# A gate product computed by four seven-product chains, with residual and embedding stored apart

## The chip, the cores and the metric

The kernel runs on one core of a Trainium2 chip. The metric is the device time of one execution in microseconds (us), the median of several executions. Before the change it is 1686.71 us (three executions, 1683.85 to 1688.95).

TensorE (PE) multiplies and accumulates into PSUM, which has eight banks of 128 x 512 float32. VectorE (DVE), ScalarE (ACT) and GpSimd (POOL) do the elementwise work. SyncE (SP) issues all DMAs here. The engines run side by side and wait for each other by semaphores.

## The reference

One layer of an encoder, with x of 1024 tokens by 1024 channels. The first sub-layer (a gated recurrence and an attention, both projected and merged) ends in `x1`. What the change concerns comes after that:

```python
x1  = layer_norm(DN_ALPHA * x + merged @ w_out, ln1_g, ln1_b)
up  = causal_depthwise_conv(x1 @ w_up, conv_w, conv_b)        # w_up: 1024 x 5632
c_val, c_gate = jnp.split(up, 2, axis=-1)
ffn = (jax.nn.gelu(c_gate) * c_val) @ w_down                  # 2816 x 1024
ple = (p_i @ w_pe) * jax.nn.sigmoid(x1 @ w_pg)                # w_pg: 1024 x 1024
return layer_norm(DN_ALPHA * x1 + ffn + ple, ln2_g, ln2_b)
```

`ple` is the per-layer embedding, and `sigmoid(x1 @ w_pg)` its gate.

## The kernel before

**Layout.** Activations lie transposed: a block of 128 channels on the partitions, 1024 tokens along the free axis. A matmul multiplies a 128 x 128 weight block with a 128 x 512 half of a block. Float32 accuracy comes from splitting each operand into a high part (a cast on ACT, line 87) and a low part (a subtraction on DVE, line 88), and from three matmuls for each product of blocks (`mm3`, lines 101 to 103).

**Stages around the change,** in the order of the trace (us from the start of the span):

1. `w_out_half` (784 to 875): the output projection, then `ln_gen` normalises `x1` half by half (512 tokens each). The second half's statistics are computed while `pe_part` runs.
2. `pe_part` (875 to 900): `p_i @ w_pe`, 96 matmuls, copied by ACT into eight tiles `pl`. Behind it stand the last small matmuls of the normalisation (`l11pr`, line 822). From these DVE scales the eight blocks `R(j)` of the second half (line 824), ACT applies gain and bias (line 864, in `x1_emit`), and each block is split (lines 87 and 88). The quadrants of `x1` are called 11, 12 (first 512 tokens, lower and upper four channel blocks), 21 and 22 (second 512 tokens).
3. `pg_part` (900 to 988): the gate, `x1 @ w_pg`. For each of eight channel blocks j and two token halves it accumulates eight `mm3`, 384 matmuls in all. ACT takes the sigmoid (line 931), DVE multiplies it into `pl` (line 932), adds `ALPHA * R(j)` (line 934) and SP writes the sum to DRAM as `rd[j]` (line 935). Beside it `x1_sums` makes four combinations of `x1`'s quadrants for each of four k (`s1`, `s3` on POOL, lines 876 and 878; `s2`, `s4` on DVE, lines 877 and 879) and splits them. The eight weight tiles of `w_pg` are split whole by `load_w` (line 97).
4. The chains `Up` (988 to 1411): 22 chains for `x1 @ w_up`. A chain computes a 2 x 2 arrangement of blocks with seven products (numbers 1 to 7) instead of eight, each of four `mm3` (12 matmuls). Its weight combinations are made on POOL (line 989: three subtractions and later a fourth) from two loaded tiles `ra`, `rb` into a single buffer `ta`, and each of seven weight tiles is split by ACT and DVE. `BANK` gives the PSUM bank of a product: 1, 6, 5 and 3 accumulate in one of four banks "a", 2 in one of three "b", 7 and 4 in the only bank "e". Products of neighbouring chains alternate in the list `seq`; a weight tile is formed `AHEAD` = 5 products before its use. Of the quadrants, the products use 11, 12, 22 and the four sums; 21 is used by `pg_part` alone.
5. The chains `Down` (1398 to 1616): `ffn`, in two groups of four chains. At the passage from `Up` to `Down`, `hooks` load the gated activations (`gr`, line 1109) and the residuals back from DRAM (`reload`, line 1165: `rr` from `rd`, two at a time), split them and make the sums of the new operands (`su`, `st` on POOL, lines 1143 and 1155). DVE then adds each finished product into `rr` (line 1102).
6. A last layer norm.

**Order and memory.** The order on TensorE is written out by hand; on the other engines a scheduler places each instruction in a list when the kernel is built, by its own estimate of when it is ready. Each engine and the SP queue work through their list in order. Large tiles come from one pool of 39 (`gp`: `R`, `pl`, split quadrants, sums, activations), weight tiles from a pool of 6 (`w`), raw weight tiles from 5 (`wr`), 128 x 512 temporaries from 6 (`hp`). A tile waits until the tile that had its place is done with.

Of the kernel before, what the change touches and what calls it, by code (L numbers as in the profile page):

```python
# [37 lines left out]
def layer_kernel(ctx, tc, xT, pT, w_in, w_a, w_b, w_out, w_up, w_dn, w_down, w_pe, w_pg,  # L38
# [872 lines left out]
    pp, pe_u, pl, last_pg = [], [], [], {}  # L911
# [11 lines left out]

    def pg_part(j, u, hf):
        cs = slice(hf * 512, hf * 512 + 512)
        ps = psS.tile([P, 512], F32, tag="s", name=f"pg{j}{hf}")
# [10 lines left out]
    def x1_sums(k):
        q = lambda j, hf: R(j)[:, hf * 512:hf * 512 + 512]
        sums(xf, k, q(k, 0), q(k + 4, 0), q(k, 1), q(k + 4, 1), f"x{k}")

    with tc.manual_schedule(engines={mybir.EngineType.PE}):
        w_out_half(0, {})
        l0 = ln_gen(R, 0, 512, x1_emit, "l10")
        next(l0)
        step = lambda g: (lambda: next(g, None))
        pre = {(0, 3): step(l0), (3, 2): step(l0), (4, 0): step(l0)}
        for i in range(4):
            src, lst, nm = ((pT[i], pp, f"p{i}") if i < 2 else (w_pe[i - 2], pe_u, f"pe{i}"))
            pre[i + 3, 4] = lambda src=src, lst=lst, nm=nm: lst.append(load_g(src, nm))
        wg = w_out_half(1, pre, ((w_pg[0], "pg0"), (w_pg[1], "pg1")))  # L950
        psD.release()
        psA.release()
        psS = tc.alloc_tile_pool(name="psS", bufs=4, space=PSUM, reuse_waits="tile")
        l1 = ln_gen(R, 512, 512, x1_emit, "l11")
        next(l1)
        for j in range(8):
            pe_part(j)
            if j in (1, 6, 7):
                next(l1, None)
        for k in range(4):  # L960
            x1_sums(k)
# [532 lines left out]
```

## Time and profile before

| | |
|---|---|
| median of three executions | 1686.71 us (1683.85 to 1688.95) |
| the profiled execution | 1684.51 us, of which the span from first to last instruction is 1682.7 us |
| TensorE busy | 1631.2 us (97%), mean granted clock 0.988 of full speed |
| VectorE, ScalarE, GpSimd busy | 1098.9 us (65%), 696.9 us (41%), 378.3 us (22%) |
| DMA | 123.7 MB, 74 GB/s in the mean |

A row of the profile that groups instructions gives line, engine, operation, output and inputs, shape and count, then the busy time in us and the mean of one in ns, and then the idle time of the engine just ahead of them with what ended it. Matmuls overlap in the pipeline, so the time of one (389 ns) is more than the distance from one start to the next. A granted clock of 1.00 is 2.4 GHz, 0.50 is 1.2 GHz.

### The profile page before, as it was taken

To read this page: it belongs to the slowest core of one execution; us is meant where nothing else is said; L and a number is where in the kernel's file an instruction comes from. 1 tells how busy PE (TensorE), PEld (TensorE's weight loads), DVE (VectorE), ACT (ScalarE), POOL (GpSimd) and SP (SyncE) were. 2 spreads that over 40 slices of the span, in tenths; PEclk is the share of its full clock that TensorE was granted. 3 is DMA by queue.
4 is the path that set the end of the run, shared out by engine and by line. 5 is a ranking of instruction groups with operands and counts; after the bars stand their busy time and mean duration, and the time that the engine had idled before them with its cause. 6 is when DMAs were issued, how large, how long until landed. Compare 5 with 4: busy or idle time off the path is not lost.

```text
span 1682.7 us, 21558 instructions
## 1 busy us (share of the span) xinstructions
PE 1631.2 (97%) x8388; PEld 1387.2 (82%) x8388; DVE 1098.9 (65%) x1545; ACT 696.9 (41%) x1189; POOL 378.3 (22%) x316
## 2 busy tenths in 40 slices
PE   7999999999999999999999999999999998898997
PEld 6889888889988888888878888888888886686896
DVE  5786867776576423325686647777777777767646
ACT  5555554542232321222356325554455544333313
POOL 0222222221012000000343132223322233222123
PEclk9999999999999999999999999999999998999999
DMA  6100000101011111114230132222222224331312
GB/s 229 38 26 26 26 26 26 38 26 38 27 38 38 38 50 50 51 38 164 99 127 11 65 123 76 83 80 101 75 76 88 82 103 161 135 132 69 118 43 100
DMA packets 37637, 123.72 MB, mean 74 GB/s; under 512 B 4128, under 2 KB 6816, under 8 KB 37536
## 3 DMA queue, kind: packets, MB, share of 16 engines
q1 hardware_dynamic: 37536, 122.35, 20.4%
q8 instruction: 66, 1.08, 0.3%
q14 instruction: 35, 0.29, 0.1%
HBM read 102.41 MB, written 19.92 MB: 73 GB/s over the span
## 4 chain that ended last, share of the span: by engine, by line
PE 84%; DVE 9%; issue 2%; DMA 2%; ACT 2%; POOL 1%; SPq 0%; POOLq 0%; DVEq 0%; ACTq 0%
PE sau L101 5%; PE sau L102 5%; PE sau L103 5%; PE seu L101 2%; PE seu L102 2%; PE seu L103 2%; PE av L431 2%; PE pi_gb L101 2%; PE pi_gb L103 2%; PE pi_gb L102 2%; PE pg L103 2%; PE pg L102 2%; PE pi_gt L103 2%; PE pi_gt L101 2%; PE pg L101 2%
## 5 line engine op out<-in xcount | busy, mean ns | idle before, releaser
L404 POOL TENSOR_TENSOR be<-be,f 128x127 f32<-128x127 f32 (+3 forms) x64 | 79.3, 1244 | 268.7 <-DVE f L402 232.9
L989 POOL TENSOR_TENSOR tau<-rbu 128x512 f32<-128x512 f32 x44 | 59.1, 1344 | 234.6 <-DVE w7u L88 214.1
L402 DVE TENSOR_TENSOR_SCAN f<-f 128x128 f32<-128x128 f32 (+3 forms) x64 | 90.3, 1421 | 27.9 <-ACT f L398 27.6
L398 ACT ACTIVATE f<-z 128x512 f32<-128x512 f32 (+2 forms) x96 | 47.6, 495 | 28.7 <-PE z L397 28.1
L88 DVE TENSOR_TENSOR wtl<-tr,wth 128x512 fp32r<-128x512 f32 (+1 forms) x80 | 48.9, 627 | 12.3 <-ACT wth L87 11.7
L788 POOL TENSOR_TENSOR l10sa<-r,r 128x512 f32<-128x512 f32 x1 | 1.3, 1284 | 233.3 <-DVE r L899 233.3
L87 ACT CAST wth<-tr 128x512 fp32r<-128x512 f32 (+1 forms) x80 | 43.5, 556 | 21.9 <-PE tr L420 20.4
L101 PE MATMUL pi_gb<-xh,wh_gb 128*128 128x512 f32 x128 | 51.5, 403 | 0.0
L103 PE MATMUL wo<-mm,wl_wo 128*128 128x512 f32 x128 | 50.0, 391 | 1.5 <-DVE wl_wo L97 1.5
L101 PE MATMUL wo<-mm,wh_wo 128*128 128x512 f32 x128 | 50.4, 394 | 0.0
L103 PE MATMUL pi_gb<-xh,wl_gb 128*128 128x512 f32 x128 | 50.0, 391 | 0.0
L101 PE MATMUL pg<-x,wh_pg 128*128 128x512 f32 x128 | 49.9, 390 | 0.0
L102 PE MATMUL pi_gb<-xl,wh_gb 128*128 128x512 f32 x128 | 49.9, 390 | 0.0
L102 PE MATMUL wo<-mm,wh_wo 128*128 128x512 f32 x128 | 49.8, 389 | 0.0
L103 PE MATMUL pg<-x,wl_pg 128*128 128x512 f32 x128 | 49.8, 389 | 0.0
L102 PE MATMUL pg<-x,wh_pg 128*128 128x512 f32 x128 | 49.8, 389 | 0.0
L101 PE MATMUL pi_gt<-xh,wh_gt 128*128 128x512 f32 x128 | 49.8, 389 | 0.0
L102 PE MATMUL pi_gt<-xl,wh_gt 128*128 128x512 f32 x128 | 49.8, 389 | 0.0
L103 PE MATMUL pi_gt<-xh,wl_gt 128*128 128x512 f32 x128 | 49.8, 389 | 0.0
L1056 DVE SCALAR_TENSOR_TENSOR ov<-hv,cv,ov 128x1023 f32<-128x1023 f32 x22 | 39.7, 1806 | 13.7 <-ACT ov L1055 13.7
L399 ACT ACTIVATE be<-z 128x512 f32<-128x512 f32 (+2 forms) x96 | 47.3, 493 | 2.7 <-POOL be L404 2.6
L420 PE MATMUL tr<-ident,be 128*128 128x128 f32 x288 | 45.6, 276 | 1.8 <-DVE wtl L88 1.0
(674 smaller groups left out, 5554.0 us busy)
## 6 DMA issues: line engine op xcount, KB each, us to landing
rau<-in_w_up SPq DMA_DIRECT2D x22, 512.0 KB, 3.2
rbu<-in_w_up SPq DMA_DIRECT2D x22, 512.0 KB, 3.2
gd<-og SPq DMA_DIRECT2D x22, 512.0 KB, 3.0
gr<-gd SPq DMA_DIRECT2D x22, 512.0 KB, 5.0
wr_wo<-in_w_out SPq DMA_DIRECT2D x16, 512.0 KB, 3.2
wr_gb<-in_w_in SPq DMA_DIRECT2D x8, 512.0 KB, 3.1
wr_gt<-in_w_in SPq DMA_DIRECT2D x8, 512.0 KB, 3.2
r<-in_xT SPq DMA_DIRECT2D x8, 512.0 KB, 7.8
```

The costliest lines, as they stand in the source:

```text
L87: nc.scalar.copy(out=hi, in_=src)
L88: nc.vector.tensor_tensor(out=lo, in0=src, in1=hi.bitcast(F32), op=ALU.subtract)
L101: mm(ps, lhsT=ah, rhs=bh, start=start, stop=False, skip_group_check=more)
L102: mm(ps, lhsT=ah, rhs=bl, start=False, stop=False, skip_group_check=more)
L103: return mm(ps, lhsT=al, rhs=bh, start=False, stop=stop, skip_group_check=more)
L398: nc.scalar.activation(f[:, s0:s1], z[:, :s1 - s0], AF.Sigmoid, scale=-0.125)
L399: nc.scalar.activation(be[:, s0:s1], z[:, :s1 - s0], AF.Sigmoid, scale=0.125)
L402: nc.vector.tensor_tensor_scan(out=f[:, :W][:, ::-1], data0=f[:, :W][:, ::-1], data1=f[:, :W][:, ::-1], initial=1.0, op0=ALU.mult, op1=ALU ...
L404: nc.gpsimd.tensor_tensor(out=be[:, :W - 1], in0=be[:, :W - 1], in1=f[:, 1:W], op=ALU.mult)
L420: nc.tensor.transpose(tr[:, j * P:j * P + P], ws[tt][:, sb * P:sb * P + P], ident)
L989: r, sub = self.raw, lambda o, a, b: nc.gpsimd.tensor_tensor(out=o, in0=a, in1=b, op=ALU.subtract)
L1056: nc.vector.scalar_tensor_tensor(out=o[:, 1:], in0=h[:, :T - 1], scalar=cv[:, c, 1:2], in1=o[:, 1:], op0=ALU.mult, op1=ALU.add)
```

## The change

- `pg_part` is replaced by a class `Pg` of four chains of the same kind as `Up` (chain j makes channel blocks j and j + 4): seven products of 12 matmuls each. Products 1 and 2 of all four chains run right behind `pe_part`, from weights that `load_early` fetches and splits without any combination; the other five go into `seq` ahead of and interleaved with the first `Up` chain.
- The products' sums end in the sigmoid on ACT and the multiplication into `pl` on DVE; three of the four quadrants need one more addition on DVE from PSUM. SP writes the result to a new DRAM tensor `pd`.
- The residual `ALPHA * x1` no longer goes through DVE: `x1_sums` scales each `R(j)` in place on ACT (128 x 1024) and SP writes it to `rd` early. `reload` fetches `rd[j]` and `pd[j]`, and POOL adds them (128 x 1024), eight times.
- Quadrant 21 is no longer split (four casts on ACT, four subtractions on DVE less). `x1_sums` makes all 16 sums first and splits them in the order s2, s3, s1, s4.
- `Chain.form` makes the weight combinations also when product 6 is formed first. The next chain is loaded when product 7 of a `Pg` chain (product 1 of the others) is formed.

```diff
     def x1_emit(j, cs):
...
-        xf[nm, j % 4] = X(f"x{nm}{j % 4}")
-        split_form(xf[nm, j % 4], R(j)[:, cs])
+        if nm != "21":
+            xf[nm, j % 4] = X(f"x{nm}{j % 4}")
+            split_form(xf[nm, j % 4], R(j)[:, cs])
...
-    def pg_part(j, u, hf):
-        cs = slice(hf * 512, hf * 512 + 512)
-        ps = psS.tile([P, 512], F32, tag="s", name=f"pg{j}{hf}")
-        wh, wl = unit_fm(u)
-        for k in range(KB):
-            last_pg[j, hf] = mm3(ps, wh(k), wl(k), *x1_part(k, hf), k == 0, k == KB - 1)
-        sg = H(f"psg{j}{hf}")
-        nc.scalar.activation(sg, ps, AF.Sigmoid)
-        nc.vector.tensor_tensor(out=pl[j][:, cs], in0=pl[j][:, cs], in1=sg, op=ALU.mult)
-        if hf:
-            nc.vector.scalar_tensor_tensor(out=pl[j], in0=R(j), scalar=ALPHA, in1=pl[j], op0=ALU.mult, op1=ALU.add)
-            nc.sync.dma_start(out=rd[j], in_=pl[j])
...
-            if i in (2, 7) and not self.summed:
+            if i in (2, 6, 7) and not self.summed:
...
+    class Pg(Chain):
+        def __init__(self, j):
+            super().__init__(f"p{j}", (w_pg[j], w_pg[j + 4]), 512, xf)
+            self.j = j
+
+        def load_early(self):
+            raw = WR(f"re{self.name}")
+            nc.sync.dma_start(out=raw, in_=self.srcs[0])
+            for i in (1, 2):
+                self.w[i] = W(f"w{i}{self.name}")
+                split_form(self.w[i], raw[:, 512 * i - 512:512 * i])
+
+        def evac(self, i, ps):
+            j = self.j
+            if i in (1, 6, 7):
+                s = H(f"s{i}_p{j}")
+                setattr(self, f"s{i}", s)
+                nc.scalar.copy(out=s, in_=ps)
+                return
+            s, o, h = {2: ("s1", 0, 0), 4: ("s6", 0, 1), 5: ("s7", 4, 1), 3: (None, 4, 0)}[i]
+            t = ps
+            sg = H(f"sg{i}_p{j}")
+            if s:
+                nc.vector.tensor_tensor(out=sg, in0=getattr(self, s), in1=ps, op=ALU.add)
+                t = sg
+            nc.scalar.activation(sg, t, AF.Sigmoid)
+            r = pl[j + o][:, 512 * h:512 * h + 512]
+            nc.vector.tensor_tensor(out=r, in0=r, in1=sg, op=ALU.mult)
+            if i in (4, 3):
+                nc.sync.dma_start(out=pd[j + o], in_=pl[j + o])
+
+    def x1_sums():
...
+        for k in range(4):
...
+            nc.gpsimd.tensor_tensor(out=s1, in0=a21, in1=a22, op=ALU.add)
+            nc.vector.tensor_tensor(out=s2, in0=s1, in1=a11, op=ALU.subtract)
+            nc.gpsimd.tensor_tensor(out=s3, in0=a11, in1=a21, op=ALU.subtract)
+            nc.vector.tensor_tensor(out=s4, in0=a12, in1=s2, op=ALU.subtract)
...
+            for j in (k, k + 4):
+                nc.scalar.activation(R(j), R(j), AF.Identity, scale=ALPHA)
+                nc.sync.dma_start(out=rd[j], in_=R(j))
+        for nm in ("s2", "s3", "s1", "s4"):
+            for k in range(4):
+                xf[nm, k] = X(f"x{nm}{k}")
+                split_form(xf[nm, k], tmp[nm, k])
...
+        pgs = [Pg(j) for j in range(4)]
+        for c in pgs:
+            c.load_early()
+        for j in range(8):
+            pe_part(j)
...
+        x1_sums()
+        for c in pgs:
+            c.prod(1)
+            c.prod(2)
...
         after(nc.sync.dma_start(out=rt[j], in_=rd[j]), gate)
+        ple = G(f"ple{j}")
+        after(nc.sync.dma_start(out=ple, in_=pd[j]), gate)
+        nc.gpsimd.tensor_tensor(out=rt[j], in0=rt[j], in1=ple, op=ALU.add)
...
-    seq = []
-    for n in range(len(chains) + 1):
+    seq = [(pgs[0], 6)]
+    for c, d in zip(pgs, pgs[1:]):
+        seq += [(c, 7), (d, 6), (c, 5), (c, 4), (c, 3)]
+    c, d = pgs[3], ups[0]
+    seq += [(c, 7), (d, 1), (c, 5), (d, 2), (c, 4), (d, 6), (c, 3), (d, 7)]
+    for n in range(1, len(chains) + 1):
```

## Rows read from the trace of the kernel before

**Rows 1.** The page, part 1: busy time, share of the span, instructions
```profile
PE 1631.2 (97%) x8388; PEld 1387.2 (82%) x8388; DVE 1098.9 (65%) x1545; ACT 696.9 (41%) x1189; POOL 378.3 (22%) x316
```
**Rows 2.** By stage: stretch, length, busy time of each engine (count), clock, DMA share, GB/s
```profile
900.50:987.70 87.20, 87.20 (x388) 72.20 (x387) 55.62 (x76) 34.75 (x58) 26.27 (x15) 1.00 0.19 73
```
**Rows 3.** Waits of TensorE, 860 to 1000: who for whom, us, times, longest
```profile
PE wo L103 <- DVE wl_wo L97: 1.5, 1, 1.5
```
**Rows 4.** Timeline of TensorE, ScalarE, VectorE, GpSimd, 899 to 923: start, duration, instruction
```profile
899.72 1.05 PE L822 MATMUL l11pr<-ident,l11ss 128*128 128x128 f32 x8
900.53 0.48 PE L101 MATMUL pg<-x,wh_pg 128*128 128x512 f32 x1
...
901.54 1.52 ACT L864 ACTIVATE r<-r,cl 128x512 f32<-128x512 f32 x2 [1.03 <-DVE r L824]
902.96 1.12 ACT L87 CAST x<-r 128x512 fp32r<-128x512 f32 x2
...
922.38 1.05 ACT L95 CAST wh_pg<-wr_pg 128x1024 fp32r<-128x1024 f32 x1 [3.14 <-PE pg L102]
...
900.81 3.08 DVE L824 TENSOR_TENSOR r<-r,l11pr 128x512 f32<-128x512 f32 x5 [3.62 <-PE l11pr L822]
...
907.34 1.32 POOL L876 TENSOR_TENSOR x0t<-r,r 128x512 f32<-128x512 f32 x1 [9.04 <-ACT r L864]
908.61 1.75 POOL L878 TENSOR_TENSOR x0u<-r 128x512 f32<-128x512 f32 x1
...
916.97 4.62 POOL L878 TENSOR_TENSOR x1u<-r 128x512 f32<-128x512 f32 x1 [4.91 <-DVE x0s L88]
```
**Rows 5.** Timeline of VectorE at 909.5
```profile
909.13 1.78 DVE L88 TENSOR_TENSOR x<-r,x 128x512 fp32r<-128x512 f32 x1
```
**Rows 6.** Groups on VectorE and GpSimd, 1411 to 1426
```profile
L88 DVE TENSOR_TENSOR gl<-gr,gh 128x1024 fp32r<-128x1024 f32 x3 | 6.7, 2288 | 0.0
L88 DVE TENSOR_TENSOR gs<-su,gs 128x512 fp32r<-128x512 f32 x3 | 5.1, 1761 | 0.0
...
L1143 POOL TENSOR_TENSOR su<-gr 128x512 f32<-128x512 f32 x3 | 6.0, 2025 | 0.0
L1155 POOL TENSOR_TENSOR st<-gr,gr 128x512 f32<-128x512 f32 x3 | 5.6, 1902 | 0.0
```
**Rows 7.** Tiles gr and rr: duration ns min/median/max, first and last start
```profile
L88 DVE TENSOR_TENSOR gl<-gr,gh x10: 1212/1222/2289, 1413.7 to 1602.5; 128x1024 fp32r<-128x1024 f32 x10
...
L1102 DVE TENSOR_TENSOR rr<-rr,sad x32: 673/686/690, 1405.1 to 1616.1; 128x512 f32<-128x512 f32 x32
```
**Rows 8.** Stretch 1398 to 1405, then timelines of SP, GpSimd, VectorE to 1413
```profile
1398.00:1405.00 7.00, 5.23 (x21) 3.45 (x20) 6.94 (x8) 4.12 (x8) 0.00 (x0) 1.00 0.34 123
...
1395.40 0.91 SPq L1165 DMA_DIRECT2D rr<-rd  x2
...
1408.62 1.02 POOL L989 TENSOR_TENSOR rad<-rad,tad 128x384 f32<-128x384 f32 x1 [20.33 <-DVE w2d L88]
...
1412.49 1.27 DVE L88 TENSOR_TENSOR w1d<-rad,w1d 128x384 fp32r<-128x384 f32 x1 [2.44 <-ACT w1d L87]
```
**Rows 9.** DMA issues, 1370 to 1460: KB each, median us to landing
```profile
rr<-rd SPq DMA_DIRECT2D x8, 512.0 KB, 4.3
```
**Rows 10.** Groups on GpSimd, whole span
```profile
L907 POOL TENSOR_TENSOR lpe<-wr_pe,hpe 128x1024 fp32r<-128x1024 f32 x2 | 5.6, 2838 | 0.0
```
**Rows 11.** The chain that ended last, 1406 to 1416: start, us, what
```profile
1406.87 1.15 DVE og L1050
...
1409.12 6.72 DMA gr<-gd
```
**Rows 12.** Timeline of TensorE, 1413 to 1417, and the stretch 1416 to 1423
```profile
1413.45 0.50 PE L101 MATMUL sbd<-gh,w0d 128*128 128x512 f32 x1 [2.03 <-ACT gh L87]
1416.02 0.79 PE L102 MATMUL sbd<-gl,w0d 128*128 128x512 f32 x1 [2.06 <-DVE gl L88]
...
1416.00:1423.00 7.00, 5.84 (x12) 3.73 (x13) 7.00 (x4) 2.80 (x5) 7.00 (x4) 0.50 0.00 0
```

More of the change, by code (lines that the diff above doesn't have):

```diff
@@ L908, in load_g @@
         return hi, lo
-    pp, pe_u, pl, last_pg = [], [], [], {}
+    pp, pe_u, pl = [], [], []
+    pd = dr.tile([8, P, T], F32, name="pd")
     rd = dr.tile([8, P, T], F32, name="rd")
@@ L922, in pe_part @@
             nc.scalar.copy(out=pl[j][:, hf * 512:hf * 512 + 512], in_=pe)
-    def pg_part(j, u, hf):
-        cs = slice(hf * 512, hf * 512 + 512)
-        ps = psS.tile([P, 512], F32, tag="s", name=f"pg{j}{hf}")
-        wh, wl = unit_fm(u)
-        for k in range(KB):
-            last_pg[j, hf] = mm3(ps, wh(k), wl(k), *x1_part(k, hf), k == 0, k == KB - 1)
-        sg = H(f"psg{j}{hf}")
-        nc.scalar.activation(sg, ps, AF.Sigmoid)
-        nc.vector.tensor_tensor(out=pl[j][:, cs], in0=pl[j][:, cs], in1=sg, op=ALU.mult)
-        if hf:
-            nc.vector.scalar_tensor_tensor(out=pl[j], in0=R(j), scalar=ALPHA, in1=pl[j], op0=ALU.mult, op1=ALU.add)
-            nc.sync.dma_start(out=rd[j], in_=pl[j])
[L937 to L961, printed above, removed]
-        for j, hf in ((0, 0), (1, 0), (2, 0), (0, 1), (1, 1), (2, 1)) + tuple((j, hf) for j in range(3, 8) for hf in range(2)):
-            if hf == 0 and j > 1:
-                wg.append(load_w(w_pg[j], f"pg{j}"))
-            pg_part(j, wg[j], hf)
     BANK = {1: "a", 6: "a", 5: "a", 3: "a", 2: "b", 7: "e", 4: "e"}
@@ L1058, in conv @@
             return o
+    with tc.manual_schedule(engines={mybir.EngineType.PE}):
+        w_out_half(0, {})
+        l0 = ln_gen(R, 0, 512, x1_emit, "l10")
+        next(l0)
+        step = lambda g: (lambda: next(g, None))
+        pre = {(0, 3): step(l0), (3, 2): step(l0), (4, 0): step(l0)}
+        for i in range(4):
+            src, lst, nm = ((pT[i], pp, f"p{i}") if i < 2 else (w_pe[i - 2], pe_u, f"pe{i}"))
+            pre[i + 3, 4] = lambda src=src, lst=lst, nm=nm: lst.append(load_g(src, nm))
+        w_out_half(1, pre)
+        psD.release()
+        psA.release()
+        psS = tc.alloc_tile_pool(name="psS", bufs=4, space=PSUM, reuse_waits="tile")
+        l1 = ln_gen(R, 512, 512, x1_emit, "l11")
+        next(l1)
+        pgs = [Pg(j) for j in range(4)]
[3 more added lines that the diff above has]
+            pe_part(j)
+            if j in (1, 6, 7):
+                next(l1, None)
+        x1_sums()
+        for c in pgs:
+            c.prod(1)
+            c.prod(2)
     PLAIN = {"q11": ("0", 0, "b"), "q21": ("0", 1, "e"), "q12": ("1", 0, "a"), "q22": ("1", 1, "f")}
@@ L1216, in layer_kernel @@
         seq += [(chains[m], i) for m, i in order if m >= 0]
-    chains[0].load(last_pg[5, 1])
+    pgs[0].load()
+    follow = {(c, 7): d for c, d in zip(pgs, pgs[1:] + ups[:1])}
+    follow.update({(c, 1): d for c, d in zip(chains, chains[1:])})
     def form(c, i):
@@ L1228, in layer_kernel @@
                 form(c, i)
-                if i == 1 and c is not chains[-1]:
-                    chains[chains.index(c) + 1].load()
+                if (c, i) in follow:
+                    follow[c, i].load()
             if m >= 0:
```

19 lines of the change are left out of this document (6 added, 13 removed).

## The prediction

> **What bounds the kernel now.** I read the page's first part, then the table by stage, the waits of TensorE, the timelines where a stage begins or ends, and the chain of waits where TensorE does wait. TensorE is busy 97% of the span [rows 1], so a change pays by taking matmuls away or costs by making TensorE wait. In the gate's stage, 900.5 to 987.7, TensorE is busy for all of 87.20 us at full clock, while DVE is busy 55.6 us and POOL 26.3 us [rows 2]. From 860 to 1000 its one wait of more than a microsecond is 1.5 us, ahead of this stage [rows 3]. So the gate is bound by its 384 matmuls. One costs 87.20 / 384 = 0.2271 us from start to start (the 389 ns of one matmul overlap).
>
> **What is taken away.** Four chains of seven products of 12 matmuls are 336. 384 - 336 = 48 matmuls less, 48 x 0.2271 = 10.9 us, all of it on the path. The eight residual additions on DVE (128 x 1024, 1.2 us each, like the row of that size in [rows 7]) go too, but no one waited for them. The sum is made against the profiled execution, 1684.5 us; it is 2.2 us below the median of 1686.7, which I add at the end.
>
> **The start of the stage is where this can be paid back.** Before, the first matmuls on the second token half came 72 matmuls after the normalisation, and the sums of quadrants were wanted only by the `Up` chains, 87 us later. Now eight products (96 matmuls) cover the preparation: the gate starts at 900.5 [rows 4], so the first product with a sum (s2) comes at 900.5 + 96 x 0.2271 = 922.3, and its fourth block is read 2.0 us on. The deadlines for the last block of s2, s3, s1 and s4 are 924.4, 927.1, 932.5 and 938.0 (products 1, 2, 4 and 6 of the list, 2.72 us each).
>
> What must be done till then? DVE scales the blocks from 900.8, and ACT applies the gain from 901.5, 0.71 us apart [rows 4]. Without the four casts of quadrant 21, ACT ends the fifth block at 901.5 + 4 x 0.71 + 0.81 = 905.2, and POOL can begin its sums then, 2.1 us earlier than before (907.34 [rows 4]). A sum alone on POOL takes 1.3 us (the one at 907.34 in [rows 4]); a 128 x 512 subtraction on DVE comes every 0.60 us ((3.08 - 0.68) / 4 [rows 4]). Work of both engines ahead of each deadline:
> - s2: 7 sums on POOL (9.1) and 20 operations on DVE (4 splits of quadrant 22, 7 sums, 4 splits of s2, 3 weight splits, 2 gate multiplications; 12.0): 21.1 us.
> - s3: 2 on POOL, 7 on DVE: 6.8 us more.
> - s1: 3 on POOL (weight combinations of the second chain), 7 on DVE: 8.1 us more.
> - s4: 9 on DVE: 5.4 us more.
>
> If the engines don't disturb each other, DVE has 34 operations ahead of the s1 deadline, 20.4 us, and is done at 925.6, 6.9 us early: cost nothing. But they do. A subtraction on DVE took 1.78 us beside a sum of 1.75 us on POOL [rows 4, 5], and while DVE went on undisturbed a sum on POOL took 4.62 us [rows 4]. At the passage to `Down` six operations of DVE (three of 1.22 us and three of 0.60 us alone, 5.5) and six of POOL (6 x 1.3 = 7.8) took 11.8 us together [rows 6, 7]: 0.89 of the sum of the two. Operations of DVE that read PSUM are not touched (673 to 690 ns in 32 instances [rows 7]). So the other bound is strict turns: done at 905.2 + 21.1 = 926.3 for s2, then 933.1, 941.2 and 946.6; the latest against its deadline is s1, 8.7 us. At 0.89 it is 905.2 + 0.89 x 36.0 = 937.2, 4.7 us late; the four gate multiplications in it (2.1 us at 0.89) can wait, which leaves 2.6. I take the middle of 4.7 and 2.6, because the scheduler's order is not known: **3.5 us**, bounds 0 and 8.7. A gain is excluded, since TensorE does not wait here now.
>
> ACT gains eight scalings of 128 x 1024 (1.05 us each, as the cast of that size [rows 4]) and loses four casts. From 901.5 to s1 it has 8 x 0.71 + 8.4 + 22 casts and 8 copies or sigmoids at about 0.5 us = 29.1, ending at 930.6 against 932.5. It fits, with no room. Within a chain, the bank of product 4 must be emptied during one product (2.7 us) by one DVE addition from PSUM (0.69); I cost that at nothing, because DVE is 64% busy here [rows 2].
>
> **SP.** The eight writes of `rd` move early and eight of `pd` are new; an issue takes some 0.4 us (0.91 for two [rows 8]). The weight loads behind them have at least the six products (16 us) between the loading and the use of a weight tile. Cost nothing; the SP queue would have to stand for over 10 us to cost something.
>
> **The passage to Down.** `reload` for blocks 0 and 4 was two loads, issued at 1395.4 [rows 8] and landing 4.3 us later [rows 9]. Now it is four loads and two additions on POOL of 2.8 us each [rows 10]. POOL stood idle 20.33 us till 1408.6 [rows 8], so its own time is hidden. DVE's is not: it is busy 6.94 of 7 us from 1398 to 1405 [rows 8], its addition into `rr` comes at 1405.1 [rows 7], and the chain of waits runs through DVE here: `og` at 1406.9, a load behind it, and then the work for which TensorE waits [rows 11]. Queued behind DVE's wait for the sum are these. If DVE loses both additions in full: 5.6 us. If it loses nothing: 0. By the 0.89 of [rows 6], 8.5 us of DVE's work (1400.0 to 1408.5) and 5.6 us take 12.5, 4.0 more, of which 2.4 us fall into DVE's idle time at 1412.5 [rows 8]: **1.6 us**. The other six additions come where POOL is idle and TensorE not late; cost nothing, or part of the same bound if that cover is gone.
>
> **Sum.** 1684.5 - 10.9 + 3.5 + 1.6 = 1678.7; with 2.2 us to the median, 1680.9, so **1681 us**, -0.3%. About 0.3% (5.1 us) is what a measurement of this kernel can tell from no change.
>
> **Rivals.**
> 1. Both tolls hidden. For it: the scheduler may put the splits that are wanted first ahead, and the first chain's weight combinations can be made before 900, where POOL is idle. Against: the sum of the work above. 1684.5 - 10.9 + 2.2 = 1675.8.
> 2. Strict turns at both places: 8.7 + 5.6 eat the gain. For it: the 1.78 and 1.75 us pair, each nearly as long as both alone (0.60 + 1.3). Against: the 0.89. 1684.5 - 10.9 + 14.3 + 2.2 = 1690.1. The Trainium skill, SBUF — State Buffer, section SBUF: two separate sides, speaks for this one: it calls the port pair that VectorE and GpSimd share an exclusive lock, held for a whole instruction, where the other fully blocks. By that rule the time would be the 1690.1; the pair in [rows 4, 5] agrees with it, the 0.89 in [rows 6] falls short of it.
> 3. Slower: the clock. At 1413 and 1416 two waits of 2.03 and 2.06 us within 3 us were followed by a stretch at a granted clock of 0.50 (1.2 GHz) [rows 12]; 7 us at half speed do 3.5 us of work, so a fall costs 3.5 us. Rival 2's waits of that size at 922 to 935 would bring one: 1690.1 + 3.5 = 1693.6. It decides from the point where two waits of 2 us come that close. Against: by the 0.89 the waits would be shorter and further apart.
> 4. The chains don't stream: at each of three chain borders product 7 waits for its only bank "e" behind a busy DVE, by one operation of 1.3 us. 3 x 1.3 = 3.9 on the forecast: 1684.8. Against: DVE has a third of the stage free.
>
> **How the numbers follow.** Forecast 0.42 (its own range 1678 to 1684), both tolls hidden 0.22, strict turns 0.18, clock 0.12, no streaming 0.06. The range 1674.5 to 1690.5 takes in the first three and the fourth rival, with a spread of about 1.3 us below, and leaves out the clock. Faster by over 0.3% (below 1681.6): 0.22 and 0.26 of the forecast's 0.42, together 0.48. Slower (above 1691.8): 0.12. Within: 0.40.
>
> **What would show it.** Matmuls of the gate: 336, 0.227 us apart, and the first `Up` chain's start about 10.9 us less the toll earlier. TensorE's waits at 922 to 938 with a releaser on DVE or ACT that splits s2, s3 or s1 give the first toll. DVE's operations of 128 x 512 between 905 and 935 lasting over 1.1 us beside POOL's show the turns; 0.68 us throughout would refute them. The waits of TensorE from 1398 to 1440 (now two of about 2 us at 1413 and 1416 among them [rows 12]) and the granted clock there give the second toll. The prediction is wrong if TensorE waits for a weight tile or a DMA in the gate's chains, if the first wait falls ahead of 922 (a PSUM bank not emptied), or if the passage to `Down` comes out shorter.

## The result, and the profile after

The changed kernel takes 1701.80 us (median of four, 1700.38 to 1705.22) against 1687.43 us of the kernel before on the same chip: a ratio of 1.0097 (95% interval 1.0080 to 1.0114; the two medians alone give 1.0085), **14.4 us slower**. The prediction was 1681 us, with a range up to 1690.5: wrong, in its sign too. Its costliest rival came to 1693.6, and slower had a chance of 0.12. The profiled execution took 1700.38 us, its span is 1698.6 us.

The page's first part answers to [rows 1]. There are 48 matmuls less and TensorE is busy 5.0 us less, yet the span is 15.9 us longer.

```profile
PE 1626.2 (96%) x8340; PEld 1380.0 (81%) x8340; DVE 1124.4 (66%) x1557; ACT 716.1 (42%) x1225; POOL 421.6 (25%) x340
```

**Where the time went.** Three instructions of TensorE cut the span at the same work in every kernel: the first matmul of `pe_part`, the last L101 matmul of the last `Up` chain's product 1, and the first matmul of Down's first chain that multiplies a block `gh` by `w1d` into the bank `sad`. In the rows by tile (duration min/median/max in ns, first and last start) of before, then of after:

```profile
L101 PE MATMUL pe<-hp,hpe x32: 389/389/793, 875.4 to 899.0; 128*128 128x512 f32 x32
L101 PE MATMUL sau<-x,w1u x88: 389/389/389, 987.7 to 1381.4; 128*128 128x512 f32 x88
L101 PE MATMUL sad<-gh,w1d x24: 389/389/389, 1452.8 to 1613.2; 128*128 128x512 f32 x24
...
L101 PE MATMUL pe<-hp,hpe x32: 389/389/796, 873.0 to 901.3; 128*128 128x512 f32 x32
L101 PE MATMUL sau<-x,w1u x88: 389/389/389, 988.8 to 1390.7; 128*128 128x512 f32 x88
L101 PE MATMUL sad<-gh,w1d x24: 389/389/389, 1468.8 to 1629.2; 128*128 128x512 f32 x24
```

From the first to the second (embedding, gate and `Up`) it was 1381.4 - 875.4 = 506.0 us and is 517.7. From there to the third (the passage) it was 71.4 and is 78.1. The rest was 229.9 and is 229.8. So with the 10.9 us that the matmuls saved, the first stretch pays a **toll of 517.7 - (506.0 - 10.9) = 22.6 us**, where 3.5 was forecast; the passage pays 6.7, where 1.6 was forecast. Ahead of the first cut the execution of after is 2.4 us shorter (873.0 against 875.4), which closes the sum: 22.6 + 6.7 - 10.9 - 0.1 - 2.4 = 15.9. The kernels in the table further down reach that cut anywhere from 872.5 to 878.1 us, so this difference is not put down to the change.

**The toll of the gate.** TensorE's waits from 860 to 1000 (who for whom, us, times, longest) answer to [rows 3]:

```profile
PE sap L103 <- DVE w6p L88: 6.2, 1, 6.2
PE sbp L101 <- DVE sg_p L985: 3.4, 1, 3.4
PE pe L101 <- ACT pl L909: 3.2, 1, 3.2
PE wo L103 <- DVE wl_wo L97: 1.5, 1, 1.5
PE sap L102 <- DVE xs L88: 1.4, 2, 0.7
PE sep L101 <- DVE sg_p L985: 1.3, 1, 1.3
```

All but the fourth are new, 15.5 us. Behind them the clock falls. By stretch (length, busy time of PE, PEld, DVE, ACT, POOL, then the granted clock):

```profile
889.00:897.00 8.00, 8.00 (x31) 6.47 (x31) 2.48 (x3) 4.19 (x8) 2.99 (x2) 0.84 0.00 0
...
926.00:931.00 5.00, 4.98 (x16) 3.64 (x14) 2.50 (x3) 5.00 (x8) 4.17 (x3) 0.69 1.02 403
...
938.00:945.00 7.00, 0.85 (x2) 0.75 (x3) 7.00 (x13) 7.00 (x15) 0.00 (x0) 0.84 0.00 0
945.00:951.00 6.00, 6.00 (x18) 4.68 (x18) 3.37 (x6) 1.90 (x4) 0.39 (x1) 0.62 0.44 161
```

Busy time times the missing clock is 8.00 x 0.16 + 4.98 x 0.31 + 0.85 x 0.16 + 6.00 x 0.38 = 5.2 us. Waits and clock make 20.7 of the 22.6; of the other 1.9, a clock of 0.97 over the 12.54 us busy from 873 to 889 gives 0.4, and for the rest no row stands.

Three of the waits have their cause in the lists of the other engines. **First, at 888.65,** ahead of the gate: in the kernel before GpSimd began the normalisation's L800 at 882.60, right behind ScalarE's mean. Now the first chain's four weight subtractions stand ahead of it, and ScalarE, waiting for GpSimd, leaves the copies that empty `pe_part`'s banks behind (GpSimd of before, then GpSimd, ScalarE and TensorE of after):

```profile
882.60 2.56 POOL L800 TENSOR_TENSOR r<-r,l11ms 128x512 f32<-128x512 f32 x2 [3.89 <-ACT l11ms L796]
...
883.26 1.29 POOL L933 TENSOR_TENSOR rap<-rap,tap 128x512 f32<-128x512 f32 x1
884.52 2.94 POOL L800 TENSOR_TENSOR r<-r,l11ms 128x512 f32<-128x512 f32 x2
886.27 1.86 ACT L807 ACTIVATE l11q<-r 128x512 f32<-128x512 f32 x3 [2.73 <-POOL r L800]
888.65 0.80 PE L101 MATMUL pe<-hp,hpe 128*128 128x512 f32 x1 [3.24 <-ACT pl L909]
```

**Second, at 925.45:** the addition that empties the first chain's bank of product 2 (`sg_p`) stands in VectorE's list behind all of its sums, and those take turns with GpSimd's. **Third, at 944.15:** the second chain's `w6p` is split behind all sixteen splits of the sums, in full lists of VectorE and ScalarE; and ScalarE had put a block of seven scalings ahead of its first cast of a sum:

```profile
909.26 1.77 POOL L1002 TENSOR_TENSOR xu<-r 128x512 f32<-128x512 f32 x1
909.78 6.90 DVE L88 TENSOR_TENSOR x<-r,x 128x512 fp32r<-128x512 f32 x4
916.60 3.48 DVE L1001 TENSOR_TENSOR xt<-xt,r 128x512 f32<-128x512 f32 x2
924.72 0.67 DVE L985 TENSOR_TENSOR sg_p<-s_p,sbp 128x512 f32<-128x512 f32 x1
925.45 0.62 PE L101 MATMUL sbp<-x,w2p 128*128 128x512 f32 x1 [3.37 <-DVE sg_p L985]
...
921.82 6.74 ACT L1006 ACTIVATE r<-r 128x1024 f32<-128x1024 f32 x7 [2.28 <-DVE xu L1003]
928.46 2.17 ACT L87 CAST xs<-xt 128x512 fp32r<-128x512 f32 x4
940.41 2.48 DVE L88 TENSOR_TENSOR xs<-xu,xs 128x512 fp32r<-128x512 f32 x4
943.42 0.68 DVE L88 TENSOR_TENSOR w6p<-tap,w6p 128x512 fp32r<-128x512 f32 x1
944.15 0.80 PE L103 MATMUL sap<-xs,w6p 128*128 128x512 f32 x1 [6.20 <-DVE w6p L88]
```

**The toll of the passage.** GpSimd's two additions stand beside VectorE's work on the last `Up` chain (GpSimd, VectorE, TensorE; then one stretch of it, and the whole passage before and after, with the clock):

```profile
1411.75 2.41 POOL L1190 TENSOR_TENSOR rr<-rr,ple 128x1024 f32<-128x1024 f32 x1 [14.19 <-DMA ple<-pd]
1415.94 2.74 POOL L1190 TENSOR_TENSOR rr<-rr,ple 128x1024 f32<-128x1024 f32 x1 [1.77 <-DMA ple<-pd]
1410.06 1.28 DVE L1051 SCALAR_TENSOR_TENSOR ov<-hv,cv,ov 128x1023 f32<-128x1023 f32 x1 [0.58 <-ACT ov L1050]
1411.86 3.38 DVE L1052 SCALAR_TENSOR_TENSOR ov<-hv,cv,ov 128x1022 f32<-128x1022 f32 x1
1416.37 3.38 DVE L1051 SCALAR_TENSOR_TENSOR og<-hg,cv,og 128x1023 f32<-128x1023 f32 x1
1410.58 0.79 PE L101 MATMUL sad<-g,w1d 128*128 128x512 f32 x1 [2.73 <-ACT g L87]
1415.90 0.80 PE L102 MATMUL sad<-g,w1d 128*128 128x512 f32 x1 [2.26 <-DVE g L88]
...
1412.00:1425.00 13.00, 10.74 (x33) 8.18 (x34) 12.32 (x11) 2.69 (x4) 5.20 (x3) 0.67 0.27 101
...
1381.40:1452.80 71.40, 58.99 (x221) 44.41 (x220) 59.40 (x75) 33.99 (x55) 22.53 (x14) 0.88 0.47 164
...
1390.70:1468.80 78.10, 61.75 (x221) 46.10 (x220) 60.18 (x69) 33.13 (x54) 33.42 (x18) 0.83 0.49 178
```

VectorE's operation of 1.28 us took 3.38 beside an addition, twice: 4.2 us lost. The first addition began only when `ple` had landed, at 1411.75. From cut to cut TensorE's waits are 16.3 us in all instead of 12.4, and the clock takes 61.75 x 0.17 = 10.5 us instead of 58.99 x 0.12 = 7.1: 3.9 + 3.4 = 7.3 for the 6.7 found, so about half of the toll is clock.

### The profile page after: what moved, and what is told of

Read it like the earlier page. It is cut to its first block, busy times and chain, and to the rows that moved or that the text cites. A ratio compares the mean times of both kernels' runs of the same rounds, so it can differ in the third digit from the quotient of the medians.

```text
span 1698.6 us, 21640 instructions
## 1 busy us (share of the span) xinstructions
PE 1626.2 (96%) x8340; PEld 1380.0 (81%) x8340; DVE 1124.4 (66%) x1557; ACT 716.1 (42%) x1225; POOL 421.6 (25%) x340
## 4 chain that ended last, share of the span: by engine, by line
PE 81%; DVE 10%; issue 3%; ACT 2%; POOL 2%; DMA 2%; SPq 0%; POOLq 0%; DVEq 0%; ACTq 0%
PE sau L102 5%; PE sau L101 5%; PE sau L103 5%; PE seu L102 2%; PE seu L103 2%; PE seu L101 2%; PE av L431 2%; PE pi_gb L101 2%; PE pi_gb L103 2%; PE pi_gb L102 2%; PE pi_gt L103 2%; PE pi_gt L101 2%; PE pi_gt L102 2%; PE sad L102 1%; PE wo L101 1%
## 5 line engine op out<-in xcount | busy, mean ns | idle before, releaser
L101 PE MATMUL pi_gb<-xh,wh_gb 128*128 128x512 f32 x128 | 51.5, 403 | 0.0
L101 PE MATMUL wo<-mm,wh_wo 128*128 128x512 f32 x128 | 50.4, 394 | 0.0
L101 PE MATMUL pi_gt<-xh,wh_gt 128*128 128x512 f32 x128 | 49.8, 389 | 0.0
L933 POOL TENSOR_TENSOR rau<-rau,tau 128x512 f32<-128x512 f32 x22 | 29.2, 1329 | 58.8 <-DVE w2u L88 58.8
L431 PE MATMUL av<-wtl,v 128*128 128x256 f32 (+1 forms) x160 | 33.2, 289 | 10.1 <-DVE wtl L88 10.0
L97 DVE TENSOR_TENSOR wl_wo<-wr_wo,wh_wo 128x512 fp32r<-128x512 f32 x32 | 35.9, 1157 | 10.3 <-ACT wh_wo L95 10.3
## 6 DMA issues: line engine op xcount, KB each, us to landing
rau<-in_w_up SPq DMA_DIRECT2D x22, 512.0 KB, 3.2
rbu<-in_w_up SPq DMA_DIRECT2D x22, 512.0 KB, 3.2
gd<-og SPq DMA_DIRECT2D x22, 512.0 KB, 2.9
gr<-gd SPq DMA_DIRECT2D x22, 512.0 KB, 5.0
wr_wo<-in_w_out SPq DMA_DIRECT2D x16, 512.0 KB, 3.3
wr_gb<-in_w_in SPq DMA_DIRECT2D x8, 512.0 KB, 3.2
wr_gt<-in_w_in SPq DMA_DIRECT2D x8, 512.0 KB, 3.2
r<-in_xT SPq DMA_DIRECT2D x8, 512.0 KB, 8.1
```

The source lines that it names most:

```text
L101: mm(ps, lhsT=ah, rhs=bh, start=start, stop=False, skip_group_check=more)
L431: mm(av[:, o], lhsT=v2[p][sb // 4][:, sb % 4, hd, :], rhs=wt[:, ms], start=sb == 0 and not lo, stop=b == i and s2 == 1 and lo)
L933: r, sub = self.raw, lambda o, a, b: nc.gpsimd.tensor_tensor(out=o, in0=a, in1=b, op=ALU.subtract)
```

## The experiments

Three theories of the gate's toll stood against each other. **T:** GpSimd and VectorE take turns during the sums, and that work is too long in any order. **L:** the order of the lists puts work that can wait ahead of work for which TensorE waits. **A:** ScalarE's eight scalings make the splits late. Lengths in the table are between the instructions above, in the profiled execution; the start of the gate is counted from `pe_part`'s first matmul, 25.1 us in the kernel before. Each ratio is against the kernel before on the same chip. One execution of each kernel was profiled, and the four of one kernel lie up to 12.4 us apart (e6d_dve, 1690.75 to 1703.19); a difference of a microsecond or two between two lengths decides nothing by itself. After and e1_ple_late, the same kernel up to the passage, agree to 0.2 us in the first stretch.

| kernel | gate starts after | first stretch | passage | rest | median | ratio (95%) |
|---|---|---|---|---|---|---|
| before | 25.1 | 506.0 | 71.4 | 229.9 | 1687.43 | |
| after | 29.8 | 517.7 | 78.1 | 229.8 | 1701.80 | 1.0097 (1.0080-1.0114) |
| e1_ple_late | 29.9 | 517.9 | 71.3 | 233.2 | 1698.70 | 1.0074 (1.0047-1.0100) |
| e2_gate | 25.5 | 513.5 | 78.8 | 229.7 | 1699.58 | 1.0082 (1.0067-1.0097) |
| e3_sums_dve | 31.2 | 517.5 | 80.8 | 230.1 | 1703.15 | 1.0106 (1.0086-1.0126) |
| e4_no_scale | 29.8 | 521.9 | 77.8 | 232.7 | 1707.24 | 1.0119 (1.0104-1.0134) |
| e5_order | 31.1 | 515.2 | 77.1 | 232.8 | 1699.50 | 1.0082 (1.0060-1.0105) |
| e6_all | 25.6 | 514.9 | 70.9 | 232.6 | 1695.96 | 1.0051 (1.0036-1.0066) |
| e6d_dve | 25.5 | 512.0 | 70.9 | 232.1 | 1696.30 | 1.0067 (1.0043-1.0092) |
| e7_all | 25.5 | 511.6 | 71.0 | 232.8 | 1692.06 | 1.0043 (1.0028-1.0058) |
| e9_s4late | 25.5 | 512.2 | 72.8 | 229.9 | 1695.87 | 1.0074 (1.0057-1.0091) |
| e7d_dve | 25.6 | 510.6 | 72.3 | 232.6 | 1692.23 | 1.0035 (1.0022-1.0049) |
| e11_x22 | 25.6 | 509.3 | 70.9 | 230.8 | 1688.94 | 1.0015 (1.0005-1.0025) |
| e12_late6 | 25.6 | 507.9 | 71.0 | 232.8 | 1684.99 | 0.9993 (0.9984-1.0002) |

**One part at a time**

*The embedding added later.* Its load and addition leave `reload` and go into the third chain of Down's first group.

```diff
+    def embed(j, gate):
         ple = G(f"ple{j}")
...
+             (downs[0][2], 1): lambda m: (embed(0, m), embed(4, m)),
+             (downs[0][2], 2): lambda m: (embed(1, m), embed(5, m)),
+             (downs[0][2], 6): lambda m: [embed(j, m) for j in (2, 6, 3, 7)],
```

> The changed kernel (1701.8 us), with the embedding's loads and additions moved out of the passage to Down into the middle of Down's first group (products 1, 2 and 6 of its third chain), where TensorE never waited. Theory T (the additions on GpSimd take turns with VectorE in the passage): the 6.6 us that the passage lost (9.3 us behind at the last Up chain, 15.9 at the end) come back, 1695 us, and the two VectorE operations of 3.38 us at 1411 to 1420 fall to 1.28. Rival G (the passage is late because the place of the clock's fall or the list of ScalarE moved with the changed stage before it, not because of the additions): the passage stays 6 us slower, 1701 us. The additions in the new place cost nothing under T.

The passage is back at 71.3 us: its 6.7 us are due to the loads and additions there, all of them. VectorE's two operations of 3.38 us take 1.28 and 1.27 (1413.08 and 1415.48), as T said; waits and clock are those of the kernel before, 12.3 us and 0.88. The rest is 3.4 us longer, but this can't be put on the additions alone: e4_no_scale and e5_order, which add where the changed kernel adds, have 232.7 and 232.8 too. After and e5_order wait the same 3.87 us there and are busy for as long, with the clock at 0.98 in the one and 0.95 in the other, 64.2 x 0.03 = 1.9 of the 3.0 us between them (70 us from 51.2 us behind the third cut, after and e5_order):

```profile
1520.00:1590.00 70.00, 64.14 (x275) 52.13 (x274) 50.91 (x74) 25.65 (x46) 19.17 (x17) 0.98 0.26 86
...
1521.60:1591.60 70.00, 64.20 (x269) 52.00 (x268) 48.81 (x73) 25.64 (x46) 18.33 (x17) 0.95 0.25 83
```

*The first chain's load held back* until `pe_part`'s block 5 is through, so that its subtractions come behind the normalisation.

```diff
-    pgs[0].load()
+    pgs[0].load(last_pe[5])
```

> The changed kernel with the first gate chain's weight load gated on the sixth block of the embedding's product, so that its four subtractions on GpSimd stand behind the normalisation's in GpSimd's list. Theory L (what is late is decided by the place in an engine's list): TensorE's wait of 3.24 us at 888.7 and the 8 us at a granted clock of 0.84 behind it vanish, the gate starts 4.7 us earlier (25.1 us behind the start of the embedding's product as before, not 29.8): 1697 us. Rival: the later load makes the first chain's weights late instead, so TensorE waits before its product 6: 1700 us or more.

The gate starts after 25.5 us, the wait of 3.24 is 0.21, and the first stretch is 4.2 us shorter. The other waits stay, but for the one of 1.3, now 2.5. This part of L is shown by the trace; the median, 1699.58, lies between the two forecasts, and the intervals of the two ratios overlap.

*The sums s1 and s3 on VectorE* instead of GpSimd.

```diff
-            nc.gpsimd.tensor_tensor(out=s1, in0=a21, in1=a22, op=ALU.add)
+            nc.vector.tensor_tensor(out=s1, in0=a21, in1=a22, op=ALU.add)
...
-            nc.gpsimd.tensor_tensor(out=s3, in0=a11, in1=a21, op=ALU.subtract)
+            nc.vector.tensor_tensor(out=s3, in0=a11, in1=a21, op=ALU.subtract)
```

> The changed kernel with the eight sums s1 and s3 of x1's quadrants on VectorE in place of GpSimd; nothing else. Theory T (strict turns): VectorE's 12 operations from 909.8 to 924.7, of up to 3.4 us, become 20 of 0.6 us, ready by 920; the wait of 3.4 us at 925.4 vanishes and those behind it shrink: 1692 to 1695 us. Rival L (list order): the gate's additions still stand behind all 16 sums, the weight splits behind all splits: at most 3 us come back, 1699 us or more. Rival A (ScalarE's eight scalings of 6.7 us hold up the splits): the wait at 925 vanishes, the one of 6.2 us before product 6 of the second chain stays: 1698 us.

The turns are gone and the wait for the bank with them, but the first stretch is the same (517.5): waits of 4.65 and 6.80 us for the high and the low part of the second chain's `w6p` stand in their place. The gate starts 1.4 us later here; behind its start the stretch is 486.3 us against 487.9. Turns were there, but in this order of the lists little is gained by giving VectorE eight operations more in their place.

*Without the scalings* (the line of the eight activations is left out, and with it the factor ALPHA of the residual).

> The changed kernel without the eight scalings of the residual on ScalarE, and nothing else (the factor ALPHA of the residual is left out). Theory A (the scalings, 6.7 us in one block ahead of s2's casts, are what makes the splits late): the casts of s2 begin 6 to 7 us earlier, the waits of 0.64 and 0.74 us at 931 to 933 go, the wait of 6.2 us at 944 shrinks, and the stage falls by 5 to 8 us, to 510 to 513, in sum about 1694. Theory L (order of the lists): with the casts earlier all sixteen splits of the sums stand ahead of the gate's additions and of w6 in VectorE's list, the waits for the bank and for w6 stay or grow, and the stage stays at 516 to 519, in sum 1700 to 1703.

Slower by 4.2 us in the first stretch, against A and by 2.9 more than L's upper end. Casts that come earlier put all sixteen splits of the sums ahead of the gate additions in VectorE's list, and the bank is waited for 9.06 us instead of 3.37:

```profile
931.48 2.49 DVE L88 TENSOR_TENSOR xs<-xu,xs 128x512 fp32r<-128x512 f32 x4
933.88 1.88 DVE L985 TENSOR_TENSOR sg_p<-s_p,sbp 128x512 f32<-128x512 f32 x3
934.62 0.79 PE L101 MATMUL sbp<-x,w2p 128*128 128x512 f32 x1 [9.06 <-DVE sg_p L985]
```

This is L's plainest case: with less work the gate's stage got longer, because of what moved up. (Of the 5.4 us between the medians, 2.9 may lie in the rest, where nothing was changed.)

*Another order in the text:* products 1 and 2 of the four chains ahead of the sums, and the splits of s1 and s4 behind the weights of the chain before.

```diff
-        x1_sums()
         for c in pgs:
             c.prod(1)
             c.prod(2)
+        split_sums = x1_sums()
...
+                if m in (-3, 0):
+                    split_sums("s1" if m else "s4")
```

> The changed kernel with three calls in another order in the program text, which the scheduler takes as priority: products 1 and 2 of the four chains ahead of the quadrant sums (so their additions and sigmoids come first), the splits of s1 behind the weight tile of the second chain's product 6, those of s4 behind the next ones. The same instructions. Theory L: the waits of 3.4 us (bank of product 2) and 6.2 us (weight tile w6 of the second chain) and the half clock behind them vanish, 12 to 15 us: 1687 to 1690 us. Theory T and rival A: the sum of the work is the same, so the wait only moves to the first use of s2 or s3: at most 5 us less, 1697 us or more.

The waits of 3.4 and 6.2 go, and one of 5.33 for the first cast of s2 comes; 2.5 us are gained. ScalarE's scalings are now what stands ahead:

```profile
934.01 2.00 ACT L1006 ACTIVATE r<-r 128x1024 f32<-128x1024 f32 x2
935.91 1.12 ACT L87 CAST xs<-xt 128x512 fp32r<-128x512 f32 x2
936.57 0.79 PE L101 MATMUL sap<-xs,w6p 128*128 128x512 f32 x1 [5.33 <-ACT xs L87]
```

**All of it together, step by step**

*e6_all* joins the held load, the order and the late embedding, and lets the first addition of Down multiply by ALPHA in place of the scalings:

```diff
-                nc.vector.tensor_tensor(out=r, in0=r, in1=ps, op=ALU.add)
+                nc.vector.scalar_tensor_tensor(out=r, in0=r, scalar=ALPHA, in1=ps, op0=ALU.mult, op1=ALU.add)
```

> All suspected list effects taken away at once: p0's weights are loaded only behind the embedding's last matmul; products 1 and 2 of the four chains stand ahead of the sums in the text; s1's and s4's splits stand behind the weights of the chain before; the embedding is reloaded and added in Down's third chain; no scaling of the residual on ScalarE (the first addition of Down to each half multiplies by ALPHA on VectorE, as one instruction of the length it had). Theory L with A (the toll of the gate stage is the order of the lists and the eight scalings): the stage falls from 517.7 to 497 to 502 us, the passage to 71.3, Down stays at 233, in sum about 1681 us, ratio 0.994 to 0.999 against the kernel before. Theory T (the toll is the turns that VectorE and GpSimd take during the sums, whatever the order): the 14 us in which GpSimd's eight sums of 1.74 us stand beside VectorE's eight keep the first second-half product late, the stage falls only to 505 to 509, in sum about 1687, ratio 1.000 to 1.004.

The passage and the rest came as expected. The first stretch is 514.9 us, outside both forecasts: 6.72 us are waited for the low part of the first chain's own `w6p`. VectorE splits it at 931.14, behind the splits of s2 and s3, though ScalarE's cast was there at 911.01 (ScalarE, VectorE, TensorE). By the same delay the second chain's subtractions start only at 932.66, when the first chain's `w7p` is split and lets go of the single buffer `ta`:

```profile
911.01 0.62 ACT L87 CAST w6p<-tap 128x512 fp32r<-128x512 f32 x1
931.14 0.69 DVE L88 TENSOR_TENSOR w6p<-tap,w6p 128x512 fp32r<-128x512 f32 x1
931.88 0.80 PE L103 MATMUL sap<-xs,w6p 128*128 128x512 f32 x1 [6.72 <-DVE w6p L88]
932.66 3.91 POOL L935 TENSOR_TENSOR tap<-rbp 128x512 f32<-128x512 f32 x1 [13.41 <-DVE w7p L88]
```

*e6d_dve:* as e6_all, with s1 and s3 on VectorE.

> As the kernel with all list effects taken away, and s1 and s3 of the four sums on VectorE too, so that nothing of the sums stands on GpSimd. Theory T: the last sum is ready some 3 to 5 us earlier than with GpSimd, and the stage is 3 us or more shorter than in the kernel with the sums on both engines. Theory L with A: the sums were not the last thing waited for, the stage is within 1.5 us of that kernel, in sum within 2 us of it.

The first stretch is 2.9 us shorter, the median the same: no verdict between the two.

*e7_all:* the first chain's weights 6 and 7 and the second chain's load ahead of the sums in the text; the embedding in Down's second group.

```diff
+        pgs[0].load(last_pe[5])
+        pgs[0].form(6)
+        pgs[0].form(7)
+        pgs[1].load()
         split_sums = x1_sums()
...
+             (downs[1][0], 7): lambda m: (embed(2, m), embed(6, m)),
+             (downs[1][1], 1): lambda m: (embed(3, m), embed(7, m)),
+             (downs[1][1], 7): lambda m: (embed(0, m), embed(4, m)),
+             (downs[1][2], 7): lambda m: (embed(1, m), embed(5, m))}
```

> The kernel with all list effects taken away, and two things more: the weights 6 and 7 of the first chain and the load of the second stand ahead of the sums in the text (there the second chain's subtractions on GpSimd began only at 932.7 us, when the first chain's w7 had been split behind all of the sums' splits, and TensorE waited 6.7 us for the second chain's w6); and the embedding is reloaded and added during the second group's chains of Down, where GpSimd is idle. Theory B (the single buffer of the combined weights, held until a split that stands late in VectorE's list): GpSimd's subtractions for the second chain begin at 918 to 921, the waits of 6.7 and 3.7 us go and the clock stays up behind them; the stage falls from 514.9 to 502 to 507 us. Rival V (VectorE has more to do from 903 to 935 than TensorE covers, in any order): a wait of 4 us or more for a split of the sums stands at 919 to 930 or at the first chain's fifth product, the stage falls to 510 to 513 only. Down: 229.5 to 230.5 us where the additions disturb nothing there, 233 where they cost the same wherever they stand. In sum 1682 to 1686 by B, 1690 to 1693 by V.

The wait of 6.7 us that this text gives to the second chain's w6 was the first chain's, as shown above; the edit is the same for both. No wait for a `w6p` is left and the second chain's subtractions start at 918.79, as B said; but VectorE now comes to s2's splits 8.10 us late, as V said, and 3.3 us are gained. Now the turns stand ahead of the wait:

```profile
906.55 6.90 DVE L88 TENSOR_TENSOR x<-r,x 128x512 fp32r<-128x512 f32 x4
919.09 3.46 DVE L1003 TENSOR_TENSOR xt<-xt,r 128x512 f32<-128x512 f32 x2
930.15 0.80 PE L102 MATMUL sap<-xs,w6p 128*128 128x512 f32 x1 [8.10 <-DVE xs L88]
```

*e9_s4late:* each split of s2 right behind its sum, s4's sums late.

> As the kernel before it in this call, and s4 (its sums and splits) only where the first chain's last product needs it, each s2 split right behind its sum, GpSimd's four s1 ahead of its four s3. Rival V: the first product with s2 starts without a wait and the stage is 2 to 5 us shorter than in the kernel with all four sums together. Theory B: s4's sums were not in the way, the stage is within 1 us of that kernel.

No gain (512.2, and the median is 3.8 us above that of e7_all): GpSimd got the second chain's combinations ahead of three of its four s1, and the last three splits of s2 came one by one, done from 926.5 to 936.2. With the embedding in the same place as in e7_all the rest is 229.9 us: added there, it costs nothing.

*e7d_dve:* e7_all with s1 and s3 on VectorE.

> The kernel with the order of the lists, the first chain's w6 and w7 ahead of the sums and the embedding added in the second group of Down, now with s1 and s3 of the sums on VectorE: GpSimd has no work between the first chain's subtractions and the second's. Theory T (in that order the turns between VectorE and GpSimd are what is left: 6.9 us for four splits of x, 1.7 us for one sum, and 8.1 us of waiting for s2's split): VectorE's operations take 0.68 each from 906 us on, its list is through s2's splits by 922 to 925, the wait of 8.1 falls to 2 to 4, and the stage to 504 to 507, in sum 1683 to 1687. Rival V (VectorE has too much to do in any case): the 8 sums more on VectorE cost what the turns gave, the wait stays at 6 us or more and the stage at 509 to 512, in sum 1689 to 1692.

510.6 us, V's forecast. Four splits of `x` take 2 x 1.29 us instead of 6.90, but 8 sums more go through VectorE, and the waits are still 5.3 and 2.2 for s2 and 3.0 for a bank.

*e11_x22:* that kernel with everything that the first chain needs late put late: s3's and s4's sums, and the splits of quadrant 22.

```diff
+            if nm == "s4":
+                for k in range(4):
+                    xf["22", k] = X(f"x22{k}")
+                    split_form(xf["22", k], R(k + 4)[:, hi])
```

> As the kernel before it in this call, with each s2 split right behind its sum, and what the first chain needs only later put there: s3's sums ahead of s3's splits, s4's sums and splits and the splits of x1's quadrant 22 ahead of the first chain's fourth product. Every part of the changed kernel's computation is kept. Theory T with L: nothing on VectorE stands ahead of s2's splits that is not needed, TensorE has no wait over 1.5 us in the gate stage, the clock stays up, and the stage is the 506.0 us of before less 10.9 and plus up to 4, 495 to 499; in sum 1674 to 1679, faster than the kernel before. Rival V: waits of 4 us or more in all stay for other splits, stage 500 to 505, in sum 1680 to 1686.

The wait for s2 is 0.5 us. Waits of 2.0 (s3), 2.8 and 4.0 (the banks of product 3 of the first two chains) are left; 509.3 us is past both forecasts, V being nearer.

*e12_late6:* the third and fourth chains' w6 formed four products later in the text (the expectation says three).

> The last kernel with one thing moved: the weights 6 of the third and fourth chains are made three products later in the text, behind the gate additions of the chain before. There the fourth chain's w6 split stood in VectorE's list ahead of the gate addition that frees the bank of the second chain's third product, and stalled it until that weight's load landed (4.0 us of TensorE at 962.9, with the clock at 0.93 behind it). Theory L: that wait goes and nothing takes its place, the clock stays at 1.00 from 960 to 985, the stage falls from 509.3 to 503 to 505.5, in sum 1682 to 1685, ratio 0.997 to 1.000. Rival D (the loads of the third and fourth chains' weights come too late in any order): a wait of 2 us or more for w6 or w7 of those chains takes its place at 950 to 975, the stage stays at 507 to 510, in sum 1686 to 1689.

The wait of 4.0 at 962.9 is gone, as L said, and the clock is 1.00 from 960 to 985. The median is 1684.99 us against 1686.30: level with the kernel before, the interval includes 1. The median is L's forecast; the stage, 507.9 us, is D's. The profiled execution was the slowest of its twelve (1689.10), but its rest of 232.8 can hold most of that, so it is open by how much 507.9 is too long. What is left in it, 507.9 - 495.1 = 12.8 us, are waits of 2.0, 0.5 and 3.2, 0.5 us at the start, and 5.6 us of clock, 11.8 in all. VectorE is full up to 930 and 0.89 and 0.73 busy in the two stretches behind it, which speaks for rival V:

```profile
923.00:930.00 7.00, 4.46 (x17) 3.05 (x16) 7.00 (x13) 5.58 (x11) 0.00 (x0) 0.86 0.00 0
930.00:940.00 10.00, 10.00 (x36) 8.00 (x35) 8.87 (x15) 6.96 (x14) 0.00 (x0) 0.76 0.31 105
940.00:950.00 10.00, 6.81 (x22) 5.23 (x21) 7.28 (x12) 3.74 (x8) 6.93 (x4) 0.75 0.17 55
```

4.46 x 0.14 + 10.00 x 0.24 + 6.81 x 0.25 and 0.9 from 950 to 960 (clock 0.91) make the 5.6. Whether another order would hide the rest, or VectorE has too much to do in any, is open; each step found another wait.

## Why the prediction was wrong

- **Taken away, 10.9 us:** right. 8388 - 8340 = 48 matmuls; from 951 on the chains run on at full clock with the one wait of 1.3 us (36.65 of 38 us busy from 951 to 989). That wait, at 958.75, is product 7's for the bank "e", which I had costed at nothing and rival 4 at 1.3 us for each of three borders: it came at one of them.
- **The start, 3.5 us with bounds 0 and 8.7: the step that failed.** It measured 22.6, of which 15.5 are waits and 5.2 clock. I set the sum of the work against each deadline as if every engine took its work in the order of the deadlines. The text said that the scheduler's order is not known, and then gave the order no price: the upper bound was strict turns in the best order. VectorE's list put the four splits of quadrant 22 and the eight sums ahead of one addition of 0.67 us that frees a bank, and all sixteen splits of the sums ahead of the second chain's `w6p`. The count of VectorE's work names the gate's multiplications, which "can wait", and not the additions ahead of them, which can't. The single `ta`, which the front part names, was given no step.
- **"The first chain's weight combinations can be made before 900, where POOL is idle"** stood as a point for rival 1. It was the first toll, 4.2 us by e2_gate. GpSimd has gaps there, but the normalisation's subtractions from 882.60 are on TensorE's path by way of ScalarE's list.
- **ScalarE at nothing ("it fits, with no room"):** the total fitted, the place didn't: seven scalings stood in one block ahead of the first cast. Yet taking them away alone cost 4.2 us more; their price is zero or more depending on what stands behind them.
- **The turns:** operations of 1.1 us and more beside GpSimd's were named as the sign, and are there, at the length of strict turns: 6.90 / 4 = 1.7 us beside sums of 1.74, against 0.6 alone [rows 4]. The Trainium skill, SBUF — State Buffer, section SBUF: two separate sides, calls the shared pair an exclusive lock held for the whole instruction; this trace agrees, 1.7 us for an operation of either. The 0.89 of [rows 6], by which I preferred the milder case, was no argument against it: both engines were busy for all of 1416 to 1423 [rows 12], and the plain turns of 909 to 916 come out alike, 1.74 us for a pair that takes 0.60 + 1.32 alone, 0.91. But taking the turns away, in the changed kernel's own order, gained nothing (e3_sums_dve).
- **The passage, 1.6 us with bounds 0 and 5.6:** the mechanism was right (e1_ple_late), the size not: 6.7, beyond the upper bound. VectorE lost 4.2 us, near the 4.0 that I had worked out; what failed is the 2.4 us that I took off for its idle time at 1412.5. The additions waited for their loads until 1411.75 and fell on work for which TensorE waits, 2.26 us at 1415.90, and the clock, which this term left out, took 3.4 more. That the other six additions cost nothing was right: the rest is 229.8 against 229.9.
- **Rival 3, the clock:** it was the right kind. Waits of 3.2 to 6.2 us, not of 2, were each followed by stretches at 0.84, 0.69 and 0.62; the price in the gate is 5.2 us for three falls, 1.7 each, half of the 3.5 that I took for one. It came on top of waits that no rival had.
- **What would show it:** a first wait ahead of 922 was named as a sign of being wrong. It ended at 888.65. A wait for a weight tile in the gate's chains was named too, and is the longest, 6.2 us.

## What to carry to other kernels

When a stage loses its slack, price the order of each engine's list and not only the sum of its work: for every instruction that frees a bank or finishes a weight, ask what is written ahead of it, and put in the text first what is waited for first. Work moved to an "idle" engine lands in front of something: look in that engine's timeline, not in its busy share, and follow who waits for what it delays. Taking one item off a crowded list tells little, since the next one takes its place; of the toll of 22.6 us all the edits together gave back 9.8, and with the late embedding that brought the kernel level with the one before, not ahead of it.

## What the runs showed of the hardware

- VectorE's operation of 128 x 1022 on two SBUF inputs took 3.38 us beside a GpSimd addition of 128 x 1024 (2.41 us), and 1.28 alone: a whole turn of the other engine for one operation. Operations with a PSUM input kept their length: `sg_p` took 0.68 us at 914.60 in e6_all, in the middle of a GpSimd sum of 1.75 (914.09).
- The same wait (3.87 us in Down) was followed by a mean clock of 0.98 in one kernel's execution and 0.95 in another's, with nothing changed in that stretch: two profiles can differ by some 2 us (64.2 x 0.03) by the clock alone, which is as much as several of the effects looked for here.
